# Column mean of an 8192 x 8192 matrix: one pass with larger loads and a last slab in pieces, instead of two passes with 2 MiB loads

## The chip, the cores and the metric

The kernel runs on one core of a Trainium2 chip. The metric is the device time of one execution in microseconds (us), lower is better. Times quoted are medians of the fast runs. A profile is one execution; its span is some 2 us shorter than the device time of such a run.

## The reference

```python
def setup_inputs():
    return {"x": np.random.randn(8192, 8192).astype(np.float32)}

def reference(x):
    return np.mean(x, axis=0)
```

The input is 268.4 MB of float32, the output 32 KB. Each element is used once, so this is a stream from memory with a little arithmetic beside it.

## The kernel before

The 8192 rows are 64 slabs of 128. A slab is loaded with a cast to bf16 (the write side of a load is half of its read side), and a vector of 128 entries 1/8192 is multiplied with it on TensorE, which sums over the 128 rows. PSUM, the memory that TensorE writes to, collects over the slabs; an eviction is the copy of finished sums from PSUM to SBUF, the core's on-chip memory, from where they are stored. A slab row of sums needs 16 chunks of 512 columns, and eight banks are used at one row each, so the matrix is taken in two passes of 4096 columns.

```python
slab_pool = ... bufs=6
...
for h in range(n_pass):                      # 2 passes of 4096 columns
    ...
    for s in range(n_slabs):                 # 64 slabs of 128 rows
        slab = slab_pool.tile([P, PASS_COLS], MM_DT)
        nc.gpsimd.dma_start(out=slab[:, :pw],            # 2 MiB read, 16 KiB per partition
                            in_=x[r0 : r0 + P, col0 : col0 + pw])
        last = s == n_slabs - 1
        for c in range(n_chunks):            # 8 chunks of 512
            ...
            nc.tensor.matmul(out=acc[0:1, c0 : c0 + cw], lhsT=ones,
                             rhs=slab[:, c0 : c0 + cw], start=(s == 0), stop=last)
            if last:
                ...                          # evict, ScalarE and VectorE in turn
    nc.sync.dma_start(out=out[col0 : col0 + pw], in_=res[0:1, :pw])
```

## Time and profile before

| | before |
|---|---|
| device time, median | 636.48 us (635.58 to 636.87, 13 runs; 636.08 of 5 when the prediction was made) |
| span of the profile | 633.8 us |
| loads | 128 of 2 MiB read |
| first data packet, last data packet | 2.60 us, 627.78 us: a stream of 625.2 us |
| last data packet to end of span | 6.1 us, the tail |

The stream and the tail are read from the DMA packets that the trace records: the stream goes from the start of the first data packet of the load queue to the end of its last one, and the tail is what is left to the end of the span. A packet is one entry of the trace's DMA record: one DMA engine moving one unbroken run of bytes, or the 4 B with which each engine closes a load. Data packets are those without the 4 B ones.

These are lines of the profile page of the kernel before. The digit rows have one digit per fortieth of the span, in tenths of full use; GB/s counts bytes written, so the read side is twice that; the queue line has packets, MB and the time of the packets as a share of 16 engines; the next is the chain of work that ended last, as shares of the span by engine; the last is the group of all matmuls (operation, shapes, count, busy us and mean ns, then idle time and what ended it).

```profile
span 633.8 us, 2369 instructions
...
PE 356.3 (56%) x1024; PEld 106.6 (17%) x1024; DVE 5.2 (1%) x9; ACT 5.8 (1%) x10; POOL 67.9 (11%) x132
...
DMA  8999999999999999999999999999999999999995
GB/s 174 215 215 215 215 215 216 216 216 216 215 216 215 215 217 216 216 216 216 216 216 215 215 215 215 216 215 216 216 215 215 216 216 216 215 215 217 215 216 119
...
q0 software_dynamic: 18432, 134.23, 101.5%
...
DMA 89%; PE 8%; issue 2%; DVE 0%; POOL 0%; DVEq 0%; POOLq 0%
...
L58 PE MATMUL acc<-slab,ones 128*1 128x512 bf16 x1024 | 356.3, 511 | 273.7 <-DMA slab<-in_x_dram 273.7
...
```

The load queue is busy in every slice, and moves the same 215 to 217 GB/s in all inner ones. TensorE works 56% of the time and waits for loads in the rest. The waits view of the kernel before (engine, line, what it waited for: us in total, times, longest) shows both sides of that:

```profile
...
POOL slab L50 <- PE acc L58: 525.6, 121, 8.2
...
PE acc L58 <- DMA slab<-in_x_dram: 273.7, 128, 8.9
...
```

GpSimd, which issues the loads, waits for TensorE to free a buffer most of the time, but that wait is harmless: while it waits, the other buffers' loads are in the queue and the DMA row shows no gap. Six buffers of 2 MiB are enough. What bounds this kernel is the load stream, plus the few us before and after it.

The timeline of the end (start, us, engine, line, operation; in brackets the idle time before and its releaser):

```profile
...
628.13 1.89 PE L58 MATMUL acc<-slab,ones 128*1 128x512 bf16 x8 [1.27 <-DMA slab<-in_x_dram]
...
628.55 2.01 ACT L67 COPY res<-acc 1x512 f32<-1x512 f32 x4 [308.21 <-PE acc L58]
628.76 2.47 DVE L69 COPY res<-acc 1x512 f32<-1x512 f32 x4 [308.09 <-PE acc L58]
631.33 0.21 SPq L70 DMA_DIRECT2D out_dram<-res  x1
```

The last slab's matmuls start at 628.13 us, just after it lands. Eight matmuls and eight evictions take until 631.23 us (628.76 + 2.47), then the output is stored and the span ends at 633.8 us.

### The profile page before, as it was taken

What the parts mean: (1) busy time and instruction counts of PE and PEld (TensorE: products, weight loads), DVE (VectorE), ACT (ScalarE), POOL (GpSimd) and SP (SyncE); (2) the same over time, 40 slices, a digit from 0 to 9 for tenths busy, and PEclk for the clock granted to TensorE, in tenths of its full rate; (3) what the DMA queues carried; (4) which work ended last, traced back from release to release, by engine and by line L of the source; (5) the groups of instructions that cost most, each with busy time, mean ns of one, the idle gap of its engine ahead of it and who ended that gap; (6) DMA issues with size and microseconds to landing.
All of it is one profiled execution on the core that took longest, in us unless ns stands there. A gap on an engine that the chain in (4) does not pass through costs nothing.

```text
span 633.8 us, 2369 instructions
## 1 busy us (share of the span) xinstructions
PE 356.3 (56%) x1024; PEld 106.6 (17%) x1024; DVE 5.2 (1%) x9; ACT 5.8 (1%) x10; POOL 67.9 (11%) x132
## 2 busy tenths in 40 slices
PE   3655675655556555554566556665655455455564
PEld 1111121111111111111111111111111111111111
DVE  0000000000000000000010000000000000000001
ACT  0000000000000000000010000000000000000001
POOL 2010011110110101101000110111001101000000
PEclk9676767587877777878786767767887878777858
DMA  8999999999999999999999999999999999999995
GB/s 174 215 215 215 215 215 216 216 216 216 215 216 215 215 217 216 216 216 216 216 216 215 215 215 215 216 215 216 216 215 215 216 216 216 215 215 217 215 216 119
DMA packets 18446, 134.41 MB, mean 212 GB/s; under 512 B 2050, under 2 KB 2050, under 8 KB 2050
## 3 DMA queue, kind: packets, MB, share of 16 engines
q0 software_dynamic: 18432, 134.23, 101.5%
q8 instruction: 8, 0.13, 0.1%
q1 hardware_dynamic: 4, 0.03, 0.0%
q14 instruction: 2, 0.02, 0.0%
HBM read 268.44 MB, written 0.03 MB: 424 GB/s over the span
## 4 chain that ended last, share of the span: by engine, by line
DMA 89%; PE 8%; issue 2%; DVE 0%; POOL 0%; DVEq 0%; POOLq 0%
DMA slab<-in_x_dram 89%; PE acc L58 8%; DVE res L69 0%; POOL slab L50 0%; DVEq L96 0%; POOLq L96 0%; POOLq L50 0%; POOLq L85 0%
## 5 line engine op out<-in xcount | busy, mean ns | idle before, releaser
L58 PE MATMUL acc<-slab,ones 128*1 128x512 bf16 x1024 | 356.3, 511 | 273.7 <-DMA slab<-in_x_dram 273.7
L58 PEld LDWEIGHTS <-ones 128*1 128x1 bf16 x1024 | 106.6, 104 | 522.9 <-issue 465.8
L50 POOL DMA_DIRECT2D slab<-in_x_dram x128 | 67.7, 530 | 534.7 <-PE acc L58 525.6
L69 DVE COPY res<-acc 1x512 f32<-1x512 f32 x8 | 5.1, 674 | 625.3 <-PE acc L58 625.3
L67 ACT COPY res<-acc 1x512 f32<-1x512 f32 x8 | 4.3, 573 | 624.0 <-PE acc L58 624.0
L37 ACT ACT_TABLE_LOAD x1 | 1.3, 1283 | 0.7 <-PEq L85 0.7
L37 ACT CAST ones<-ones_f 128x1 bf16<-128x1 f32 x1 | 0.2, 194 | 0.0
L85 POOL MEMSET const-float32-0.0<- 128x1 f32 x1 | 0.1, 99 | 0.2 <-issue 0.2
L85 POOL MEMSET const-bfloat16-1.0<- 128x1 bf16 x1 | 0.1, 102 | 0.0
L85 POOL MEMSET const-float32-1.0<- 128x1 f32 x1 | 0.1, 99 | 0.0
L85 POOL MEMSET const-uint8-127<- 128x1 uint8 x1 | 0.1, 99 | 0.0
L35 DVE MEMSET ones_f<- 128x1 f32 x1 | 0.1, 59 | 0.8 <-PEq L85 0.8
## 6 DMA issues: line engine op xcount, KB each, us to landing
slab<-in_x_dram POOLq DMA_DIRECT2D x128, 1024.0 KB, 25.8
out_dram<-res SPq DMA_DIRECT2D x2, 16.0 KB
```

The lines of the kernel that those rows point to most:

```text
L35: nc.vector.memset(ones_f32, 1.0 / R)
L37: nc.scalar.copy(out=ones, in_=ones_f32)
L50: nc.gpsimd.dma_start(out=slab[:, :pw], in_=x[r0 : r0 + P, col0 : col0 + pw],)
L58: nc.tensor.matmul(out=acc[0:1, c0 : c0 + cw], lhsT=ones, rhs=slab[:, c0 : c0 + cw], start=(s == 0), stop=last,)
L67: nc.scalar.copy(out=res[0:1, c0 : c0 + cw], in_=acc[0:1, c0 : c0 + cw])
L69: nc.vector.tensor_copy(out=res[0:1, c0 : c0 + cw], in_=acc[0:1, c0 : c0 + cw])
L85: nc = _bacc.Bacc("TRN2", target_bir_lowering=False, num_devices=1)
```

## The change

Its intent is to feed the DMA engines with fewer, larger loads and to shorten the end. Sixteen chunks of sums are now kept in PSUM at once, half of them at partition 32 of the same banks, so one pass is enough. A load takes two slabs: partition p reads rows 2p and 2p+1, 64 KiB in one run. There are four buffers, each four times as large as one before. The last slab comes in eight pieces of 1024 columns, each evicted and stored by itself. The factor 1/8192 moves from the ones vector into the eviction.

```diff
-    slab_pool = ctx.enter_context(tc.tile_pool(name="slab", bufs=6))
+    slab_pool = ctx.enter_context(tc.tile_pool(name="slab", bufs=4))
...
+    def chunk_psum(c):
+        b, q = c % BANKS, c // BANKS
+        return acc[QROWS[q] : QROWS[q] + 1, b * CHUNK : b * CHUNK + cw]     # QROWS = (0, 32, ..)
...
+    SPD = 2                     # slabs per load
+    TAIL_SINGLES = 3            # then three loads of one slab
...
+        slab = slab_pool.tile([P, SPD * C], MM_DT)
+        src = x[g0 * P : (g0 + ns) * P, :]
+        if ns > 1:
+            nc.gpsimd.dma_start(
+                out=slab[:, : ns * C].rearrange("p (k c) -> p k c", c=C),
+                in_=src.rearrange("(p k) c -> p k c", k=ns))
+        else:
+            nc.gpsimd.dma_start(out=slab[:, :C], in_=src)
+        for k in range(ns):
+            for c in [h + BANKS * q for h in range(BANKS) for q in range(n_q)]:   # 0, 8, 1, 9, ..
+                nc.tensor.matmul(out=chunk_psum(c), lhsT=ones, rhs=slab[:, k*C+c0 : k*C+c0+cw], ...)
...
+    for pi, cs in enumerate(pieces):                     # last slab: 8 pieces of 2 chunks
+        nc.gpsimd.dma_start(out=last[:, p0:pend], in_=row[:, p0:pend])
+        for c in cs: nc.tensor.matmul(..., stop=True)
+        for c in cs: ...                                  # nc.scalar.mul or nc.vector.tensor_scalar by 1/R
+        nc.sync.dma_start(out=out[p0:pend], in_=res[0:1, p0:pend])
```

More of the change, by code (lines that the diff above doesn't have):

```diff
@@ L20 @@
     assert R % P == 0, "row count must be a multiple of 128"
-    CHUNK = 512
-    NBANK = 8
-    PASS_COLS = NBANK * CHUNK
     n_slabs = R // P
     MM_DT = mybir.dt.bfloat16
+    CHUNK = 512
+    BANKS = 8
+    QROWS = (0, 32, 64, 96)
+    n_chunks = (C + CHUNK - 1) // CHUNK
+    n_q = (n_chunks + BANKS - 1) // BANKS
+    assert n_q <= len(QROWS), "input too wide for a single pass"
+    inv_r = 1.0 / float(R)
     const_pool = ctx.enter_context(tc.tile_pool(name="const", bufs=1))
-    slab_pool = ctx.enter_context(tc.tile_pool(name="slab", bufs=6))
+    slab_pool = ctx.enter_context(tc.tile_pool(name="slab", bufs=4))
@@ L31 @@
     psum_pool = ctx.enter_context(tc.tile_pool(name="acc", bufs=1, space=bass.MemoryType.PSUM))
-    res_pool = ctx.enter_context(tc.tile_pool(name="res", bufs=2))
+    res_pool = ctx.enter_context(tc.tile_pool(name="res", bufs=1))
     ones_f32 = const_pool.tile([P, 1], mybir.dt.float32)
-    nc.vector.memset(ones_f32, 1.0 / R)
+    nc.vector.memset(ones_f32, 1.0)
     ones = const_pool.tile([P, 1], MM_DT)
     nc.scalar.copy(out=ones, in_=ones_f32)
-    n_pass = (C + PASS_COLS - 1) // PASS_COLS
@@ L40 @@
-    for h in range(n_pass):
-        col0 = h * PASS_COLS
-        pw = min(PASS_COLS, C - col0)
-        n_chunks = (pw + CHUNK - 1) // CHUNK
-        acc = psum_pool.tile([P, PASS_COLS], mybir.dt.float32)
-        res = res_pool.tile([P, PASS_COLS], mybir.dt.float32)
-        for s in range(n_slabs):
-            r0 = s * P
-            slab = slab_pool.tile([P, PASS_COLS], MM_DT)
+    acc = psum_pool.tile([P, BANKS * CHUNK], mybir.dt.float32)
+    res = res_pool.tile([1, C], mybir.dt.float32)
@@ new lines, in chunk_psum, with chunk_cols @@
+    def chunk_psum(c):
+        b, q = c % BANKS, c // BANKS
+        cw = min(CHUNK, C - c * CHUNK)
+        return acc[QROWS[q] : QROWS[q] + 1, b * CHUNK : b * CHUNK + cw]
+    def chunk_cols(c):
+        cw = min(CHUNK, C - c * CHUNK)
+        return c * CHUNK, cw
+    SPD = 2
+    TAIL_SINGLES = 3
+    bulk = n_slabs - 1
+    groups = []
+    s0 = 0
+    while s0 < max(0, bulk - TAIL_SINGLES):
+        ns = min(SPD, bulk - TAIL_SINGLES - s0)
+        groups.append((s0, ns))
+        s0 += ns
@@ L50 @@
+    while s0 < bulk:
+        groups.append((s0, 1))
+        s0 += 1
+    for g0, ns in groups:
+        slab = slab_pool.tile([P, SPD * C], MM_DT)
+        src = x[g0 * P : (g0 + ns) * P, :]
+        if ns > 1:
             nc.gpsimd.dma_start(
-                out=slab[:, :pw],
-                in_=x[r0 : r0 + P, col0 : col0 + pw],
-            )
-            last = s == n_slabs - 1
-            for c in range(n_chunks):
-                c0 = c * CHUNK
-                cw = min(CHUNK, pw - c0)
+                out=slab[:, : ns * C].rearrange("p (k c) -> p k c", c=C),
+                in_=src.rearrange("(p k) c -> p k c", k=ns),
+            )
+        else:
+            nc.gpsimd.dma_start(out=slab[:, :C], in_=src)
+        for k in range(ns):
+            s = g0 + k
+            for c in [h + BANKS * q for h in range(BANKS) for q in range(n_q)]:
+                c0, cw = chunk_cols(c)
@@ L58 @@
                 nc.tensor.matmul(
-                    out=acc[0:1, c0 : c0 + cw],
+                    out=chunk_psum(c),
                     lhsT=ones,
-                    rhs=slab[:, c0 : c0 + cw],
+                    rhs=slab[:, k * C + c0 : k * C + c0 + cw],
                     start=(s == 0),
-                    stop=last,
+                    stop=False,
                 )
-                if last:
-                    if c % 2 == 0:
-                        nc.scalar.copy(out=res[0:1, c0 : c0 + cw], in_=acc[0:1, c0 : c0 + cw])
-                    else:
-                        nc.vector.tensor_copy(out=res[0:1, c0 : c0 + cw], in_=acc[0:1, c0 : c0 + cw])
@@ L70 @@
-        nc.sync.dma_start(out=out[col0 : col0 + pw], in_=res[0:1, :pw])
+    s = n_slabs - 1
+    last = res_pool.tile([P, C], MM_DT)
+    row = x[s * P : (s + 1) * P, :]
+    pieces = []
+    for b in range(BANKS):
+        cs = [c for c in range(b * n_q, min((b + 1) * n_q, n_chunks))]
+        if not cs:
+            continue
+        pieces.append(cs)
+    for pi, cs in enumerate(pieces):
+        p0, _ = chunk_cols(cs[0])
+        pend = chunk_cols(cs[-1])[0] + chunk_cols(cs[-1])[1]
+        nc.gpsimd.dma_start(out=last[:, p0:pend], in_=row[:, p0:pend])
+        for c in cs:
+            c0, cw = chunk_cols(c)
+            nc.tensor.matmul(
+                out=chunk_psum(c),
+                lhsT=ones,
+                rhs=last[:, c0 : c0 + cw],
+                start=(s == 0),
+                stop=True,
+            )
+        for c in cs:
+            c0, cw = chunk_cols(c)
+            src_ap = chunk_psum(c)
+            dst_ap = res[0:1, c0 : c0 + cw]
+            if c % 2 == 0:
+                nc.scalar.mul(out=dst_ap, in_=src_ap, mul=inv_r)
+            else:
+                nc.vector.tensor_scalar(
+                    out=dst_ap,
+                    in0=src_ap,
+                    scalar1=inv_r,
+                    scalar2=None,
+                    op0=mybir.AluOpType.mult,
+                )
+        nc.sync.dma_start(out=out[p0:pend], in_=res[0:1, p0:pend])
```

## The prediction

> **What bounds it now.** The page's queue table shows the load queue busy for 101.5% of the 16 DMA engines' span, and the slice view shows 215 to 217 GB/s written in every slice but the first and the last. The destination is bf16 and the source float32, so the read side runs at twice that. By the timeline, TensorE starts its first slab at 8.89 us and its last at 628.13 us, 127 loads of 2 MiB apart, or 4.876 us each: 430 GB/s read. TensorE is busy 356 us of 634 and waits 273.7 us for loads (waits view); GpSimd waits 525.6 us for buffers, but with six in flight no slice shows the DMA engines starved. So the bound is the transfer itself. [...]
>
> **Outside the stream.** Head: about 3 us before the engines are full (first slice 174 instead of 215 GB/s). Tail: from the last landing at 628.13 us, 5.7 us: eight matmuls and evictions to 631.2, then the output.
>
> **What the change does.** It moves the same bytes. 128 loads of 2 MiB become 30 of 8 MiB, 3 of 4 MiB and 8 of 0.5 MiB. Each partition's source run grows from 16 KiB to 64 or 32 KiB. Matmuls stay 1024 of 128x512; half now write partition 32 of a bank. The end of pass one (near 317 us) goes; the slices there show 216 GB/s, so it cost nothing. The last slab is cut so that only two matmuls and one eviction per engine follow the last landing.
>
> **Costs.**
> - Stream: [...] The last slab's 4 KiB runs may give back up to 1 us. I take 2 us saved, all critical.
> - Tail: eight matmuls (1.89 us) and a queue of four evictions per engine (2.47 us on VectorE) shrink to two matmuls and one eviction (0.67 us): about 1.5 us saved, all critical.
> - Load issue on GpSimd is 530 ns each; larger loads may take more, but each has 19 us of transfer to hide in.
> - TensorE: a pair of slabs needs 32 matmuls. At the cold spacing seen (427 ns) that is 13.7 us, under the 19.5 us that 8 MiB take to load. [...]
> - Buffers: four of 8 MiB hold more in flight than six of 2 MiB, so no starving.
>
> Total: 636.1 - 2 - 1.5 = about 632.5 us. Range 628.8 to 637.0. Faster by over 2%: 0.03; within 2%: 0.93; slower by over 2%: 0.04.
>
> **What would show it.** Right: DMA share 9 in all inner slices, 215 to 218 GB/s; data packets fewer by half or more; the chain still nearly all load; last landing to end of span about 4 us; TensorE idle on loads. Wrong: a slice under 213 GB/s; chain with a large TensorE share.
>
> **What would make it wrong.** [...] the last 0.5 MiB loads running well below the stream's rate; or a real rate limit above the 430 GB/s that I read as the ceiling.

Where a cut is marked, the prediction rested on a ceiling of the rate, or on ways of going wrong, that no trace or run shows. The sum: 636.1 us, less 2 for the stream and 1.5 for the tail, about 632.5 us. "Cold" means the slower of the two spacings of matmuls in the trace of the kernel before, 427 and 215 ns.

## The result and the profile after

The kernel after takes 629.91 us (629.41 to 629.96, 7 runs) against 636.48 us. The ratio is 0.9897 (95% interval 0.9887 to 0.9907). Ratios are the mean time of one kernel's fast runs over that of the other's of the same rounds, so they are not quite the ratio of the medians quoted. A gain of 6.6 us is clear of the noise.

The same lines of the page after, and its chain line:

```profile
span 627.7 us, 2203 instructions
...
PE 191.3 (30%) x1024; PEld 59.4 (9%) x1024; DVE 5.3 (1%) x9; ACT 6.0 (1%) x10; POOL 22.0 (4%) x45
...
DMA  9999999999999999999999999999999999999997
GB/s 192 209 221 213 222 211 223 211 221 212 215 219 207 228 206 228 207 228 207 227 209 226 209 226 210 223 211 223 211 222 213 221 213 220 215 220 215 210 217 144
...
q0 software_dynamic: 5904, 134.22, 99.8%
...
another core or an unknown queue 62%; PE 26%; DMA 8%; issue 2%; POOL 1%; DVE 0%; POOLq 0%
...
L82 PE MATMUL acc<-slab,ones 128*1 128x512 bf16 x1008 | 186.8, 551 | 431.0 <-DMA slab<-in_x_dram 431.0
...
L106 PE MATMUL acc<-last,ones 128*1 128x512 bf16 x16 | 4.7, 413 | 2.5 <-DMA last<-in_x_dram 2.5
...
```

The load queue still fills every slice; it moves the same 134.22 MB written in 5904 packets instead of 18432, and these take 99.8% instead of 101.5% of a span that is itself shorter. The GB/s row swings more than before because a packet is now 32 KiB written (nearly 2.5 us) and is booked to the slice in which it starts. TensorE's busy time nearly halves, and nothing comes of it. The chain of waits puts 62% to "another core or an unknown queue": on one core that cannot be another core, and the gaps so named are those in which TensorE waits for a load, as the waits view says. That makes about 70% of load in the chain, for 89% before, and TensorE's share rises from 8% to 26%; e8 below tests whether that share matters:

```profile
...
POOL slab L72 <- PE acc L82: 497.4, 26, 26.1
PE acc L82 <- DMA slab<-in_x_dram: 431.0, 33, 23.5
...
```

The timeline of the end:

```profile
...
624.21 0.59 PE L106 MATMUL acc<-last,ones 128*1 128x512 bf16 x2 [0.62 <-DMA last<-in_x_dram]
624.39 1.42 SPq L127 DMA_DIRECT2D out_dram<-res  x2
624.62 0.59 ACT L118 ACTIVATE res<-acc 1x512 f32<-1x512 f32 x1 [0.62 <-PE acc L106]
624.84 0.68 DVE L120 TENSOR_SCALAR res<-acc 1x512 f32<-1x512 f32 x1 [0.53 <-PE acc L106]
```

After the last piece's landing there are two matmuls, one eviction on each engine until 625.52 us, and a 4 KB store. In the packets of the trace the two profiles compare like this:

| | before | after | difference |
|---|---|---|---|
| first data packet | 2.60 | 2.59 | 0.0 |
| stream | 625.2 | 621.3 | -3.9 |
| last packet to first matmul of it | 0.36 | 0.32 | 0.0 |
| that matmul to end of last eviction | 3.10 | 1.31 | -1.8 |
| end of last eviction to end of span | 2.6 | 2.2 | -0.4 |
| span | 633.8 | 627.7 | -6.1 |

So the question is twofold: whether the tail is worth its 2.2 us by itself, and what made the stream 3.9 us shorter, with the same bytes and an already full queue.

### The profile page after: what moved, and what is told of

Read it like the earlier page. It is cut to its first block, busy times and chain, and to the rows that moved or that the text cites. A ratio compares the mean times of both kernels' runs of the same rounds, so it can differ in the third digit from the quotient of the medians.

```text
span 627.7 us, 2203 instructions
## 1 busy us (share of the span) xinstructions
PE 191.3 (30%) x1024; PEld 59.4 (9%) x1024; DVE 5.3 (1%) x9; ACT 6.0 (1%) x10; POOL 22.0 (4%) x45
## 3 DMA queue, kind: packets, MB, share of 16 engines
q0 software_dynamic: 5904, 134.22, 99.8%
## 4 chain that ended last, share of the span: by engine, by line
another core or an unknown queue 62%; PE 26%; DMA 8%; issue 2%; POOL 1%; DVE 0%; POOLq 0%
PE acc L82 26%; DMA slab<-in_x_dram 7%; DMA last<-in_x_dram 2%; POOL last L103 1%; DVE res L120 0%; POOL slab L72 0%; PE acc L106 0%; POOL slab L77 0%; POOLq L153 0%; POOLq L142 0%
## 5 line engine op out<-in xcount | busy, mean ns | idle before, releaser
L82 PE MATMUL acc<-slab,ones 128*1 128x512 bf16 x1008 | 186.8, 551 | 431.0 <-DMA slab<-in_x_dram 431.0
L82 PEld LDWEIGHTS <-ones 128*1 128x1 bf16 x1008 | 58.2, 111 | 558.6 <-issue 541.2
L72 POOL DMA_DIRECT2D slab<-in_x_dram x30 | 16.0, 534 | 498.2 <-PE acc L82 497.4
L120 DVE TENSOR_SCALAR res<-acc 1x512 f32<-1x512 f32 x8 | 5.2, 677 | 619.5 <-PE acc L106 619.4
L118 ACT ACTIVATE res<-acc 1x512 f32<-1x512 f32 x8 | 4.5, 583 | 618.5 <-PE acc L106 618.4
L103 POOL DMA_DIRECT2D last<-in_x_dram x8 | 4.2, 541 | 38.1 <-DMA slab<-in_x_dram 38.1
L106 PE MATMUL acc<-last,ones 128*1 128x512 bf16 x16 | 4.7, 413 | 2.5 <-DMA last<-in_x_dram 2.5
L77 POOL DMA_DIRECT2D slab<-in_x_dram x3 | 1.6, 527 | 56.4 <-PE acc L82 56.4
L106 PEld LDWEIGHTS <-ones 128*1 128x1 bf16 x16 | 1.2, 93 | 6.3 <-DMA last<-in_x_dram 4.5
```

Of the source, the lines that this page charges most:

```text
L72: nc.gpsimd.dma_start(out=slab[:, : ns * C].rearrange("p (k c) -> p k c", c=C), in_=src.rearrange("(p k) c -> p k c", k=ns),)
L77: nc.gpsimd.dma_start(out=slab[:, :C], in_=src)
L82: nc.tensor.matmul(out=chunk_psum(c), lhsT=ones, rhs=slab[:, k * C + c0 : k * C + c0 + cw], start=(s == 0), stop=False,)
L103: nc.gpsimd.dma_start(out=last[:, p0:pend], in_=row[:, p0:pend])
L106: nc.tensor.matmul(out=chunk_psum(c), lhsT=ones, rhs=last[:, c0 : c0 + cw], start=(s == 0), stop=True,)
L118: nc.scalar.mul(out=dst_ap, in_=src_ap, mul=inv_r)
```

## The experiments

For the stream there are three candidates: fewer packets (1024 data packets per engine before, 328 after), fewer loads (128 and 41), and another order over memory (half rows before, whole rows after). Packets and loads fell by the same factor, so the two kernels alone cannot tell them apart. All kernels below gave correct results. They ran on three chips: e1, e2, e3 and e7 on one, e4, e5, e6 and e8 on a second, e9 to e11 and the second run of the kernel after on a third; the kernel before went along with each set and took 636.55, 636.05 and 636.66 us. First the numbers together; loads and packets are counted from the trace.

| kernel | loads | data packets per engine | stream us | tail us | median us | ratio to before |
|---|---|---|---|---|---|---|
| before | 128 | 1024 | 625.2 | 6.1 | 636.5 | 1 |
| after | 41 | 328 | 621.3 | 3.8 | 629.9 | 0.9897 |
| after, run again | 41 | 328 | 621.7 | 3.8 | 629.5 | 0.9892 |
| e1 tail only | 131 | 1048 | 625.4 | 3.7 | 633.6 | 0.996 |
| e2 tail whole | 34 | 272 | 621.4 | 12.2 | 637.3 | 1.0014 |
| e7 order | 128 | 1024 | 625.2 | 7.3 | 636.0 | 0.9997 |
| e3 runs of 16 KiB | 41 | 1072 | 624.0 | 3.8 | 632.3 | 0.9935 |
| e4 runs of 8 KiB | 41 | 2080 | 627.4 | 3.8 | 636.0 | 0.9996 |
| e5 runs of 4 KiB | 41 | 4096 | 634.4 | 3.8 | 643.6 | 1.0116 |
| e6 loads of 1 MiB | 256 | 2048 | 631.4 | 5.3 | 641.1 | 1.0075 |
| e8 column order | 41 | 328 | 621.7 | 3.8 | 629.5 | 0.9895 |
| e9 loads of 16 MiB | 26 | 328 | 620.9 | 10.4 | 636.2 | 0.9998 |
| e10 finer end | 42 | 336 | 621.4 | 4.0 | 629.9 | 0.9898 |
| e11 both | 27 | 336 | 621.5 | 10.5 | 636.8 | 1.0005 |

Five profiles of kernels with the loads of the kernel after or close to it (after twice, e2, e8, e10) have streams of 621.3 to 621.7 us, so a stream is good to about 0.4 us, across the three chips.

### e1: the new tail on the kernel before

```diff
+            step = 1024 if (last and h == n_pass - 1) else pw
+            for q0 in range(0, pw, step):
                 nc.gpsimd.dma_start(out=slab[:, q0 : q0 + step], in_=x[r0 : r0 + P, col0 + q0 : col0 + q0 + step])
...
+                    if h == n_pass - 1 and c % 2 == 1:      # store two chunks at a time
+                        nc.sync.dma_start(out=out[...], in_=res[0:1, c0 - CHUNK : c0 + cw])
...
```

> The kernel before with the new tail alone: the last slab of pass two in four loads of 0.5 MiB, evicted and stored piece by piece. Theory (the tail is worth 2.2 us of the 6.1 us by which the span shrank): about 2 us faster than the kernel before, 634.3 us; from last landing to end of span 3.8 us instead of 6.1, the stream no shorter, perhaps 0.2 us longer. Rival (all of the gain comes from the stream): no change, 636.4 us.

It took 633.59 us, ratio 0.996 (0.9947 to 0.9972). The stream stayed (625.4 us), the tail fell to 3.7 us. In its timeline, the last two matmuls and the eviction after them:

```profile
...
628.34 0.59 PE L60 MATMUL acc<-slab,ones 128*1 128x512 bf16 x2 [0.36 <-DMA slab<-in_x_dram]
...
628.76 0.57 ACT L69 COPY res<-acc 1x512 f32<-1x512 f32 x1 [0.28 <-PE acc L60]
```

By the profiles the tail is worth some 2.3 us alone, on the old loads; by the ratio, 2.5 us (1.8 to 3.4 by its interval). The remaining 4 us of the change are the stream's.

### e2: the new loads without the pieces

```diff
-    for b in range(BANKS):
-        cs = [c for c in range(b * n_q, min((b + 1) * n_q, n_chunks))]
-        ...
-        pieces.append(cs)
+    pieces.append(list(range(n_chunks)))
```

> The kernel after with the last slab as one load of 4 MiB, sixteen matmuls and evictions after it, one output. Theory: 3 to 6 us slower than the kernel after (632.9 to 635.9 us), because the tail now holds 16 matmuls of 0.2 to 0.43 us and eight evictions per engine; the stream 0.3 to 0.5 us shorter, as the short pieces go. Rival (tail worth nothing): 629.5 us.

It took 637.31 us, ratio 1.0014: the whole gain of the change is gone, and it lies above the range that I gave. The tail is 12.2 us. Its timeline shows why I had it too short:

```profile
...
624.26 4.82 PE L102 MATMUL acc<-last,ones 128*1 128x512 bf16 x16 [6.10 <-DMA last<-in_x_dram]
...
627.87 4.06 ACT L114 ACTIVATE res<-acc 1x512 f32<-1x512 f32 x8 [625.64 <-PE acc L102]
627.91 4.97 DVE L116 TENSOR_SCALAR res<-acc 1x512 f32<-1x512 f32 x8 [627.04 <-PE acc L102]
...
632.97 0.31 SPq L123 DMA_DIRECT2D out_dram<-res  x1
```

The evictions come behind all matmuls of a piece in the program. I had thought of them running beside the matmuls, as they do in the kernel before, but the first starts at 627.87 us, 3.6 us after the first matmul, and eight of them per engine then take 5 us. It did not wait for all sixteen matmuls: three had yet to start (628.01, 628.44 and 628.70 us). The other half of the expectation, a stream 0.3 to 0.5 us shorter, did not show: it is 621.4 us, within the scatter. One pass doubles the last slab's work (16 chunks instead of 8), so with big loads the pieces at the end are not a refinement: without them the tail eats the whole gain of the stream.

### e3, e4, e5: the loads of after, in more packets

A gap of 256 B in the buffer after each part of a row breaks a partition's run, and with it the packet; loads, order and matmuls stay. H is 2, 4 and 8 (e5 has three buffers instead of four).

```diff
-        slab = slab_pool.tile([P, SPD * C], MM_DT)
+        slab = slab_pool.tile([P, SPD * H, C // H + 128], MM_DT)
...
-                out=slab[:, : ns * C].rearrange("p (k c) -> p k c", c=C),
-                in_=src.rearrange("(p k) c -> p k c", k=ns),
+                out=slab[:, : ns * H, : C // H],
+                in_=src.rearrange("(p k) (h c) -> p (k h) c", k=ns, h=H),
...                                # single slabs and matmuls indexed to match
```

> The kernel after with its 41 loads, but gaps in the destination so that each source run is 16 KiB as before, 1072 data packets per engine instead of 328. If a packet costs time (5.6 ns each, from 3.9 us saved over 696 fewer packets per engine): stream 4.2 us longer, about 634.1 us. If a load costs time (45 ns each) or the order over memory does: no change, 629.9 us.

> As the 16 KiB run, with source runs of 8 KiB: 41 loads, 2080 data packets per engine. If a packet costs 5.6 ns: stream 9.8 us longer than the kernel after's, about 639.7 us. If loads or order set the time: 629.9 us.

> As the 16 KiB run, with source runs of 4 KiB: 41 loads, 4096 data packets per engine [...]. If a packet costs 5.6 ns: stream 21 us longer than the kernel after's, about 651 us. If loads or order set the time: 629.9 us.

The slice row and the load queue of each, from the DMA view:

```profile
...
GB/s 168 216 216 216 216 216 216 216 216 217 216 216 216 216 216 216 216 216 215 217 216 216 216 216 216 216 216 216 217 216 216 216 216 216 216 217 216 215 216 145
...
q0 software_dynamic: 17808, 134.22, 101.9%
...
```

```profile
...
GB/s 163 215 215 215 215 215 215 215 215 215 215 215 215 215 215 215 215 215 214 215 215 215 215 215 215 215 215 215 215 215 215 215 215 215 215 215 215 214 215 148
...
q0 software_dynamic: 33936, 134.22, 105.0%
...
```

```profile
...
GB/s 158 212 212 212 213 212 212 212 212 213 212 212 213 212 213 212 213 213 213 213 213 212 213 212 212 213 212 212 213 212 213 212 213 213 212 213 213 213 212 150
...
q0 software_dynamic: 66192, 134.22, 110.7%
...
```

The times are 632.25, 635.96 and 643.57 us. A packet does cost time: the inner slices fall from 216 to 215 to 212 and 213 GB/s as the packets grow in number, at the same loads and the same bytes. From e3 to e4 the stream grows by 3.45 us over 1008 packets per engine, from e4 to e5 by 7.03 us over 2016: 3.4 and 3.5 ns per packet, a straight line. From the kernel after to e3 it is 2.7 us over 744, 3.6 ns (3.0 with the stream of its second profile; of these runs only e4 and e5 share a chip). But that is less than the 5.6 ns of the packets-only theory: packets alone explain 696 times 3.5 ns, or 2.4 us, of the 3.9 us. And e3, which has slightly more packets than the kernel before, still has a stream 1.2 us shorter. Something else counts too.

### e6: more loads, in the packets of e4

The kernel before with each load cut in two by columns.

```diff
-            nc.gpsimd.dma_start(out=slab[:, :pw], in_=x[r0 : r0 + P, col0 : col0 + pw])
+            for q0 in range(0, pw, 2048):
+                nc.gpsimd.dma_start(out=slab[:, q0 : q0 + 2048],
+                                    in_=x[r0 : r0 + P, col0 + q0 : col0 + q0 + 2048])
```

> The kernel before with every load cut in two by columns: 256 loads of 1 MiB, runs of 8 KiB, 2048 data packets per engine. Its packets are those of the 8 KiB run, with 256 loads for 41. If packets alone cost 5.6 ns: stream 5.7 us longer than before's, the same as the 8 KiB run's stream within 1 us. If loads alone cost 45 ns: also 5.7 us longer than before's, but 9.7 us longer than the 8 KiB run's stream.

```profile
...
GB/s 170 213 213 214 213 214 214 214 214 214 213 214 213 214 214 213 213 213 214 213 214 213 213 214 213 214 213 213 213 213 213 213 214 214 213 213 214 214 214 131
...
q0 software_dynamic: 36864, 134.23, 104.7%
...
```

It took 641.07 us. Over its stream that is 425 GB/s read (268.4 MB in 631.4 us); the 2 MiB loads of the kernel before ran at 429 and the kernel after, mostly 8 MiB loads, at 432 GB/s. The data packets are nearly those of e4 (2048 for 2080 per engine), but the stream is 4.0 us longer, with 256 loads for 41. So packets alone fail here by 4.0 us, and loads alone, which called for 9.7 us, by 5.7 us. Allowing 0.1 us for the 32 packets, a load costs 4.1 us / 215 = 19 ns. The pair before and e3 gives the same in another place: 1.2 us, and 0.2 us for 48 packets more in e3, over 87 loads: 16 ns. With a scatter of 0.4 us per stream the first is good to some 2 ns, the second to some 5.

The packets in the traces show both costs directly. Median data packets of 2, 4, 8, 16 and 32 KiB written took 173, 324, 625, 1227 and 2432 ns: 75.3 ns per KiB and 22 ns on top. Of the 16384 data packets of the kernel before, 16369 have another packet that starts 18 to 20 ns before they end, so that 3 to 4 ns of the 22 remain as the cost of a packet. The trace kept here does not name the engine of a packet, but 30 ns further off only 56 have such a neighbour. A load ends with one packet of 4 B per engine, recorded with 22 ns. 2047 of the 2048 of the kernel before also start 18 to 20 ns before the end of a data packet, and 2034 have a data packet that starts 20 to 23 ns after them (none has one at 50 to 53 ns). So that packet holds up the next load by 21 to 22 ns, which is the cost of a load. By these spacings 87 loads and 696 packets fewer save about 4.3 us. The profiles give 3.9 and 3.5. Packets that took longer than the median of their size cost 0.5 us per engine before and 1.1 and 1.4 us in the two profiles after, about as much as is missing; what slows them was not looked into.

The buffers differ too (six of 2 MiB, four of 8 MiB), but the queue runs dry in neither: leaving out the first 10 and the last 15 us of the stream, the 16 engines stand idle for 0.36 us on average before and 0.38 us after. (With 256 loads GpSimd waits 474 us in all for earlier loads to land before it issues the next; the DMA row of e6 is still 9 in all inner slices and its engines stand idle for 0.22 us by the same count, so that wait is harmless.)

### e7: the order over memory

The kernel before with its loads, but both halves of a slab one after the other, sums of the second half at partition 32.

```diff
-    for h in range(n_pass):
-        ...
-        for s in range(n_slabs):
+    for s in range(n_slabs):
+        for h in range(n_pass):
...
-                    out=acc[0:1, c0 : c0 + cw],
+                    out=acc[32 * h : 32 * h + 1, c0 : c0 + cw],
```

> The kernel before with its 128 loads of 2 MiB and 16 KiB runs, but one pass: both halves of a slab are loaded one after the other, so memory is read in order as in the kernel after. If the order over memory made the stream faster: about 4 us faster than before, 632.5 us. If packets or loads did: the stream as before, 625.2 us, and the time within 0.5 us of 636.4.

```profile
...
q0 software_dynamic: 18432, 134.23, 101.3%
...
```

It took 636.02 us, ratio 0.9997 (0.9984 to 1.0009); the stream is 625.2 us, as before. Reading memory in whole rows, and with it the single pass as such, is worth nothing here. It also removes the evictions and the store from the middle of the kernel, which shows that they cost nothing there. Its tail is 7.3 us instead of 6.1, because the last eight matmuls took 3.57 us in this profile:

```profile
...
628.13 3.57 PE L59 MATMUL acc<-slab,ones 128*1 128x512 bf16 x8 [1.87 <-DMA slab<-in_x_dram]
...
```

In the profile of the kernel before they took 1.89 us. All slabs of both kernels show either kind, or a mixture, by whether TensorE runs at 0.43 or 0.21 us per matmul at that moment. That is probably why the runs of the kernel before spread over 1.3 us (635.54 to 636.83 in one set of nine) and those of the kernel after over 0.6: the profile of before that is compared here is one of the quick ones (span 633.8 us, others up to 635.1), and the 6.1 us between the two profiles are a little less than the 6.6 us between the medians.

### e8: TensorE's order

```diff
-            for c in [h + BANKS * q for h in range(BANKS) for q in range(n_q)]:
+            for c in range(n_chunks):
```

> The kernel after with the matmuls of a slab in column order, so that neighbours write the same partition of PSUM. Theory (TensorE off the critical path): time unchanged within 0.5 us; TensorE busy back up from 191 us to about 350 us, because pairs on partitions 0 and 32 no longer run at the same time. Rival (the freed TensorE helps the stream): some us slower.

The lines for TensorE from its page:

```profile
...
PE 221.4 (35%) x1024; PEld 73.4 (12%) x1024; DVE 5.2 (1%) x9; ACT 5.8 (1%) x10; POOL 22.0 (4%) x45
...
L82 PE MATMUL acc<-slab,ones 128*1 128x512 bf16 x1008 | 218.0, 524 | 401.8 <-DMA slab<-in_x_dram 401.8
...
```

The time is 629.53 us, 629.50 for the kernel after run again: no effect, as expected of an engine off the critical path, though TensorE's share of its chain is 30%. The second half of the expectation missed. TensorE's busy time rose from 191 to 221 us only, not to 350. The order accounts for 30 us of the 165 us that the change took off it. That matmuls pair up in the kernel after is in its trace: before the last slab the program writes partitions 0 and 32 in turn, and all 504 pairs of such neighbours start within 8 ns of each other, while pairs follow at about 427 or 215 ns. That they cannot pair up in column order was the author's guess. e7, with both partitions in use but bursts of eight matmuls, has 353.0 us. So what is left comes with the bursts of 32. The starts of the matmuls in the trace show two parts of that: a burst begins at 0.43 us per step and goes over to 0.21 us after some 3.5 to 6 us, so that a longer burst runs more of its matmuls at the fast rate; and in e8 too, pairs start within 0.05 us of each other after the first four, though all but a few neighbours in the program write the same partition. How the 135 us divide between the two was not tried.

### e9, e10, e11: can it be better still

e9 takes four slabs per load and two buffers (SPD = 4, bufs=2). e10 cuts the last piece into two of one chunk and shares the last eviction:

```diff
+    pieces = pieces[:-1] + [[c] for c in pieces[-1]]
...
+            if c == n_chunks - 1:
+                nc.scalar.mul(out=dst_ap[:, :hw], in_=src_ap[:, :hw], mul=inv_r)           # hw = 256
+                nc.vector.tensor_scalar(out=dst_ap[:, hw:], in0=src_ap[:, hw:], ...)
```

e11 is both. The kernel after went along as a yardstick.

> The kernel after, unchanged, as a yardstick on this chip: 629.9 us, stream 621.3 us, tail 3.8 us.

> The kernel after with loads of 16 MiB (four slabs, two buffers): 15 of them for 30. From the runs so far a load costs 16 to 19 ns and a packet about 3.5 ns. If packets stay at 64 KiB read (128 KiB runs cut in two): 0.3 us off the stream, 629.6 us. If a packet grows to 128 KiB: 120 fewer packets per engine, another 0.4 us. Rival (the cost is one of starting and draining, so longer loads help more): over 1 us faster.

> The kernel after with the last of its eight pieces cut into two of 512 columns and the last eviction shared by ScalarE and VectorE, 256 columns each. One matmul and a half-size eviction fewer after the last landing: tail 0.3 to 0.5 us shorter (3.3 to 3.5 us), stream at most 0.1 us longer: 629.5 us. Rival (the tail is the output store alone): 629.9 us or a little more.

> 16 MiB loads and the finer end together: if both add up, about 0.7 us faster than the kernel after, 629.2 us.

The yardstick took 629.50 us, e9 636.20 us, e10 629.90 us and e11 636.83 us. None beats the kernel after.

The stream of e9 is 620.9 us, some 0.4 to 0.8 us shorter than that of the kernel after: near what 15 fewer loads at 16 to 19 ns would give (0.3 us), within the scatter of a stream. e11, with the same loads, has 621.5 us, so a gain is not shown. Its data packets are still 328 per engine, and the largest wrote 32 KiB: a run of 128 KiB is cut in two. What spoils e9 is the tail of 10.4 us. On GpSimd, which issues the loads, its timeline shows

```profile
...
556.12 0.56 POOL L77 DMA_DIRECT2D slab<-in_x_dram  x1 [39.07 <-PE acc L82]
556.67 3.20 POOL L103 DMA_DIRECT2D last<-in_x_dram  x6
...
595.11 0.53 POOL L77 DMA_DIRECT2D slab<-in_x_dram  x1 [9.38 <-DMA slab<-in_x_dram]
596.81 0.53 POOL L77 DMA_DIRECT2D slab<-in_x_dram  x1 [1.18 <-PE acc L82]
...
```

With two buffers only one of the three single slabs (L77) found a free one at 556 us. Six pieces of the last slab, which have a buffer of their own, went out at once, and the other two singles had to wait until 595 and 597 us. So the last two whole singles landed with only one piece behind them, and TensorE did the work of two slabs at the end:

```profile
...
613.07 3.40 PE L82 MATMUL acc<-slab,ones 128*1 128x512 bf16 x16 [16.56 <-DMA slab<-in_x_dram]
622.72 3.58 PE L82 MATMUL acc<-slab,ones 128*1 128x512 bf16 x16 [6.24 <-DMA slab<-in_x_dram]
626.08 3.70 PE L106 MATMUL acc<-last,ones 128*1 128x512 bf16 x16
```

The order in which the loads go out comes from when buffers come free, not from the order of the source alone. e11 inherits this. Four slabs per load without the single slabs at the end were not tried.

e10 missed as well: its tail is 4.0 us, not 3.3 to 3.5.

```profile
...
624.27 0.38 PE L107 MATMUL acc<-last,ones 128*1 128x512 bf16 x1 [0.27 <-DMA last<-in_x_dram]
624.68 0.37 ACT L120 ACTIVATE res<-acc 1x256 f32<-1x256 f32 x1
625.09 0.42 DVE L121 TENSOR_SCALAR res<-acc 1x256 f32<-1x256 f32 x1 [0.80 <-ACT res L120]
```

The two halves of the last eviction did not run side by side. VectorE waited 0.80 us and its releaser is ScalarE, so the halves (0.37 and 0.42 us) took turns, and were no faster than one whole eviction on each engine from two banks. The trace names what held it: VectorE's half waits for the semaphore that ScalarE's half raises, a dependence set in the program. Whether the two could read one bank at once is not shown. The eviction is not where e10 lost time, though: from the first matmul to the end of the last eviction it took 1.24 us, for 1.31 in the kernel after. From there to the end of the span it took 2.47 us for 2.17, with one more store, of 2 KB; why is open.

## Why the prediction was right or wrong

The range (628.8 to 637.0) and the verdict (within 2%) held, the range near its lower end. The point, 632.5 us, was 2.6 us too high, because both savings were sized too small.

- **"So the bound is the transfer itself."** Right. Every kernel's time follows stream plus tail. e8, which changes TensorE alone, changes nothing.
- **"I take 2 us saved, all critical."** The right direction, mis-sized. It measured 3.9 us (3.5 with the second profile of the kernel after). The 2 us were a guess; e3 to e6 show what it should have been made of. At the measured 75.3 ns per KiB written, on 16 engines, a load of 2 MiB read would take 4.819 us; by the prediction's count from the trace of the kernel before it took 4.876 us, 57 ns more. Of these, eight packets at 3.5 ns and one load at 16 to 19 ns make up 44 to 47 ns. At the same 75.3 ns, an estimate from the packets of these traces, all 134.2 MB written would take 616.9 us. Packets and loads account for 5.8 of the 8.3 us that the stream takes beyond that before, and 1.9 of 4.4 us after; some 2.5 us stay in both. As a rate, 75.3 ns per KiB on each of 16 engines is 435 GB/s read. What sets it is not shown.
- **"The last slab's 4 KiB runs may give back up to 1 us."** Less. Eight pieces are 56 packets per engine and seven loads more than one whole load (328 and 272, 41 and 34): by the rates above 0.3 us. e2, which removes them, has a stream within the scatter.
- **"Tail: ... about 1.5 us saved."** Right in kind, too small: 2.3 us. Evictions gave 1.8 us. The 4 KB store at the end instead of 16 KB gave 0.4 us, of which I had not thought: its packet took 0.16 us instead of 0.61, and e1, with 4 KB on the old loads, also ends 2.1 us after its last eviction.
- **"The end of pass one ... cost nothing."** Right; e7 takes it away and the stream is the same to 0.1 us.
- **"TensorE: ... 13.7 us."** Too high, and it did not matter. A pair of slabs took 5 to 6.5 us.
- **The checks.** DMA share 9 in all inner slices: held. "The chain still nearly all load" against "chain with a large TensorE share": neither, with 70% and 26%. This was no sign of error; e8 has 30% and the same time. "215 to 218 GB/s" in every slice and "a slice under 213 GB/s" as a sign of error: a bad check, as single slices swing from 206 to 228 with packets of 2.5 us. The mean over the stretches 50 to 200, 200 to 400 and 400 to 600 us is 216, 217 and 216. "Data packets fewer by half or more": held (16384 to 5248). "Last landing to end of span about 4 us": held (3.8).

## What to carry to other kernels

The stream here already filled its queue (DMA row at 9 in all inner slices), and what could still be gained was overhead per packet and per load (3.9 us of stream) and work after the last landing (2.3 us of tail). In such a case count packets and loads per engine, and multiply by what an experiment measures for each (here 3.5 ns for a packet, and 16 to 22 ns for a load), before hoping for more. In this kernel larger loads make the tail longer unless the last of them is cut small, so the two belong together: the large loads without the pieces (e2, a tail of 12.2 us) gained nothing. And after a change to loads or buffers, look at the order in which the loads really went out, because the end of the kernel depends on which of them land last, as e9 showed with its tail of 10.4 us.
